# A fused encoder layer on one core: the S5 tap products issued strip by strip, or round the four column strips

## The chip, the cores and the metric

The kernel runs on one core of a Trainium2 chip (trn2). A core has five engines that run side by side, each in the order of its own instruction stream: TensorE (PE in the profile, with PEld for its weight loads), VectorE (DVE), ScalarE (ACT), GpSimd (POOL) and SyncE (SP), which only issues DMAs here. They wait for each other through semaphores. The metric is the time of one execution on the device in microseconds (us).

## The reference, cut to what matters

The layer has a parallel mixer (an S5 state-space branch and a gated MLP branch, merged by gates), cross-attention to 256 memory tokens, and a SwiGLU feed-forward part, for 512 tokens of width 1024. The change is in the S5 branch:

```
def s5_scan(u, lam_re, lam_im, log_step, b_re, b_im, c_re, c_im, reverse):
    lam = lax.complex(lam_re, lam_im)
    step = jnp.exp(log_step)[:, None]
    lam_bar = jnp.exp(lam * step)
    b_bar = ((lam_bar - 1.0) / lam)[..., None] * b
    bu = jnp.einsum('gpc,lbgc->lbgp', b_bar, u)
    _, states = lax.associative_scan(_linear_recurrence, (a, bu), axis=0, reverse=reverse)
    return jnp.einsum('gcp,lbgp->lbgc', c, states).real

y = d * u
for direction, reverse in ((0, False), (1, True)):
    y = y + s5_scan(u, ..., reverse)
y = gelu(y); y = y * sigmoid(y @ w_glu)
```

There are 32 groups of 16 channels, each with 64 complex states and two directions.

## The kernel before, in words

**Stages.** The dense products of the layer are cut into blocks of weights of 512 KB. Each block is loaded into `wraw` (SP), split into two parts `whi` and `wlo` by ScalarE and VectorE (`split`, L83 to L89), and multiplied on TensorE in three products per pair (`mm3`, L355; `product`, L1101). A plan (`next_w`, L330) loads blocks a few steps ahead. In order: the projections of the input (tiles `pt` and `pf`), the merge products (`bx`, `bq`, `qv`), GLU, output projection, attention, feed-forward.

**The S5 branch beside it.** It is a generator (`s5_program`, L937) that is advanced by `tick` (L453) after each block of dense products, so that its small work on VectorE, ScalarE and GpSimd is traced between the dense blocks. Work that is to come a little later is put off with `later(n, fn)` (L443), n counted in steps of 5.2 us. The sequence is split into 64 chunks of 8 steps. Within a chunk, the branch is a convolution with 15 taps of 16 x 16 per group; across chunks, a scan (`s5_scan`, L893) carries the states.

**The taps.** The 32 groups are taken in four octets of 8 groups. For an octet, `s5_kernels(o)` (L781) lets VectorE form two tiles `e`, the real part (i = 0) and the imaginary part (i = 1), each 128 partitions (64 states x 2 directions) by 8 groups by 8 steps by 16 channels (L790 to L797). Then `products()` (L800) runs:

- GpSimd clears two tiles `bd` (L804), ScalarE copies the input matrices in (L807).
- TensorE forms the taps in a PSUM tile `pk` of 128 x 2 x 128 (L809 to L819). The octet has two quads (q) of four groups (j). Group j of a quad writes only the 32 PSUM partitions from 32j on, with weights of 32 columns, that is one of four column strips of the array (`tile_position=(0, 32 * j)`). Per group there are four products in plain fp32: a wide one (128 columns of `e`, L814) for i = 0 and i = 1, and a narrow one (16 columns, L817) for i = 0 and i = 1, which adds one tap of the other direction on top. All four add into the same strip, the first with `start`, the last with `stop`.
- `store` (L822) copies the taps to `ks` on ScalarE (L827), adds the skip term on VectorE (L828). `spill` (L831) writes them to DRAM as `kd` by DMAs of SP and GpSimd (L835, L836), and `load` (L839) reads them back as `tt` in another arrangement by eight DMAs (L843; on GpSimd's queue for octets 0 and 1, on SP's for 2 and 3).

`s5_outputs(o)` (L904) needs `tt` and the scanned states: ScalarE copies the states to `ss` (L916, L917), TensorE forms `py` (L922 to L924), ScalarE applies the GELU to `y` (L929), and eight DMAs store `yd` (L932). The tiles `tt`, and `y` with `ks`, have one buffer each; `e`, `bd` and `ss` have two. `s5_inputs` (L851) uses transposes (`pw`, L864) and products (`pz`, L871) on the way to the scan. In the program's order the octets 0 and 1 have their taps before the scan; octet 2's are formed after the outputs of octet 0, octet 3's after those of octet 1.

**Who sets the order.** A scheduler orders each engine's instructions when the kernel is built, by its own timing model: an instruction whose operands it takes to be ready may go ahead of others that were traced earlier, or fall behind them. `in_order` (L93, `keep_in_program_order`) ties an instruction behind the instruction of its engine that was traced just before it. It fixes the order of issue and waits for nothing. On the chip every engine then keeps the order that was built. Before the change the tap products have no such tie. In the traced order an octet's first tap product stands directly behind the last dense product of the step before.

Of the kernel before, what the change touches and what calls it, by code (L numbers as in the profile page):

```python
# [27 lines left out]
C = 16  # L28
# [11 lines left out]
Q = 8  # L40
# [12 lines left out]
def hybrid_layer_kernel(  # L53
# [8 lines left out]
    nc = tc.nc  # L62
# [14 lines left out]
    def bank(name):  # L77
        return pm.tile([P, 512], F32, tag="mm", name=name)

    def aux(name, shape=(P, 512)):  # L80
        return pa.tile(list(shape), F32, tag="aux", name=name)
# [11 lines left out]
    in_order = tc.keep_in_program_order  # L93
# [349 lines left out]
    def later(n, fn):  # L443

        side["later"].append((side["now"] + n, fn))
# [321 lines left out]
    def inner(t, gs, n):  # L767

        return t[:, gs, :].unsqueeze(3).to_broadcast([P, GO, t.shape[2], n])

    def outer(t, gs, n):

        return t[:, gs, :].unsqueeze(2).to_broadcast([P, GO, n, t.shape[2]])

    def lc(t, g):
        return t[:, g].rearrange("p a b -> p (a b)")

    def glc(t):
        return t.rearrange("p g a b -> p (g a b)")

    def s5_kernels(o):  # L781

        gs = slice(o * GO, (o + 1) * GO)
        cr, ci = st["c"]
        pr, pi = st["pe"]
        es = []
        for i in range(2):
            e = s5p.tile([P, GO, Q, C], F32, tag="e%d" % i, name="e%d" % i, bufs=2)
            w = s5p.tile([P, GO, Q, C], F32, tag="etmp", name="etmp")
            V.tensor_tensor(e, outer(cr, gs, Q), inner((pr, pi)[i], gs, C), ALU.mult)  # L790
            yield 1.1
            V.tensor_tensor(w, outer(ci, gs, Q), inner((pi, pr)[i], gs, C), ALU.mult)
            yield 1.1
            if i == 0:
                V.tensor_tensor(e, e, w, ALU.subtract)
            else:
                V.scalar_tensor_tensor(glc(e), glc(e), -1.0, glc(w), ALU.mult, ALU.subtract)  # L797
            es.append(e)
            yield 1.1
        def products():  # L800
            bd = []
            for i in range(2):
                t = s5p.tile([P, GO, 2, C], F32, tag="bd", name="bd", bufs=2)
                nc.gpsimd.memset(t, 0.0)  # L804
                for d in range(2):
                    hf = slice(64 * d, 64 * d + 64)
                    nc.scalar.copy(t[hf, :, d, :], st["b"][i][hf, gs, :])  # L807
                bd.append(t)
            ps = aux("pk", (P, 2, P))  # L809
            for q in range(2):  # L810
                for j in range(4):
                    g = 4 * q + j
                    for i in range(2):
                        nc.tensor.matmul(ps[32 * j:32 * j + 32, q, :], bd[i][:, g].rearrange("p d c -> p (d c)"),  # L814
                                         lc(es[i], g), start=(i == 0), stop=False, tile_position=(0, 32 * j))
                    for i in range(2):
                        nc.tensor.matmul(ps[32 * j:32 * j + C, q, 0:C], bd[i][:, g, 1, :],  # L817
                                         es[i][:, g, Q - 1, :], start=False, stop=(i == 1),
                                         tile_position=(0, 32 * j))  # L819
            later(0.5, lambda: store(ps))  # L820

        def store(ps):  # L822
            ks = s5p.tile([P, 2, P], F32, tag="y", name="ks")
            dd = s5p.tile([P, 2, C], F32, tag="dd", name="dd", bufs=2)
            in_order(V.tensor_tensor(dd, st["dmask"].unsqueeze(1).to_broadcast([P, 2, C]),
                                     st["dcol"][:, 2 * o:2 * o + 2].unsqueeze(2).to_broadcast([P, 2, C]), ALU.mult))
            nc.scalar.copy(ks, ps)  # L827
            V.tensor_tensor(ks[:, :, 0:C], ks[:, :, 0:C], dd, ALU.add)  # L828
            later(0.5, lambda: spill(ks))

        def spill(ks):  # L831
            kd = dp.tile([GO, C, 15, C], F32, name=f"kd{o}")
            for j in range(4):
                kdj = kd.rearrange("(q j) c l e -> j c q (l e)", j=4)[j]
                (nc.gpsimd, nc.sync)[o > 1].dma_start(kdj[:, :, 7 * C:15 * C], ks[32 * j:32 * j + C])  # L835
                nc.gpsimd.dma_start(kdj[:, :, 0:7 * C], ks[32 * j + C:32 * j + 2 * C, :, 0:7 * C])  # L836
            later(1.2, lambda: load(kd))

        def load(kd):  # L839
            tt = s5p.tile([P, GO, P], F32, tag="tt", name="tt")  # L840
            kf = kd.rearrange("g c l e -> c g (l e)")
            for l in range(Q):
                (nc.gpsimd, nc.sync)[o > 1].dma_start(tt[l::Q], kf[:, :, (7 - l) * C:(15 - l) * C])  # L843
            st["oct", o] = (es[0], es[1], tt)

        later(1, products)
        yield 0.1

# [211 lines left out]
    for h in range(H):  # L1060
        ps = bank("psv")
# [56 lines left out]
    def unit_bank(name):  # L1118
        return bank(name).rearrange("p (j t) -> p j t", j=2)
# [367 lines left out]
    for t0 in (0, 2):  # L1487
        ps = {t: bank(f"pt{t - t0}") for t in (t0, t0 + 1)}
# [77 lines left out]
    ps = [bank("pf0"), bank("pf1")]  # L1566
# [67 lines left out]
    for i, u in enumerate(UNITS):  # L1634
        final = i == len(UNITS) - 1
        x, v = begun
        q = unit_bank("pq")
# [132 lines left out]
    for i in range(2):  # L1770
        p = aux("pcut", (P, 256))
# [37 lines left out]
```

## Time and profile before

| | us |
|---|---|
| time, median of 3 runs | 893.77 (893.14 to 894.84) |
| span of the profiled execution, first to last instruction | 891.3 |
| TensorE busy in it | 881.1 (99%) |
| VectorE busy | 642.5 (72%) |
| ScalarE busy | 487.4 (55%) |
| wide tap products (L814), 128 on the chip, first and last start | 65.1 to 290.8 |
| narrow tap products (L817), 128 on the chip, first and last start | 69.1 to 291.0 |

The profile has no separate time for the profiled execution beside its span; the median of the runs lies 2.4 us above the span. A line of the timeline gives the start and the length in us, the engine, the line of the kernel, the operation, what it writes and reads, the shape, and a count where equal neighbours are merged; brackets hold the idle time of the engine just before it and what ended it. The lengths of matrix products are modelled and overlap, so starts are what to compare.

### The profile page before, as it was taken

The numbers are of one execution on the slowest core, as the hardware profiler recorded it, in microseconds if no ns is written. First come the engines' busy times: TensorE is split into PE (matmuls) and PEld (weight loads), VectorE is DVE, ScalarE is ACT, GpSimd is POOL, SyncE is SP. The second block draws the span as 40 slices with busy tenths as digits, with TensorE's granted clock in tenths as the row PEclk, the third lists the DMA queues.
The fourth block names the chain that finished last, engine by engine and source line by source line (L and its number), as shares of the span: only waits on it lengthen the run. The fifth ranks groups of instructions, "written<-read, shape, count | busy, mean of one in ns | idle before, by whom it ended". The sixth has DMA issues, their size and how long they took to land.

```text
span 891.3 us, 14796 instructions
## 1 busy us (share of the span) xinstructions
PE 881.1 (99%) x5744; PEld 788.0 (88%) x5744; DVE 642.5 (72%) x1048; ACT 487.4 (55%) x714; POOL 106.9 (12%) x165
## 2 busy tenths in 40 slices
PE   9999999999999999999999999999999999999996
PEld 6788888888889998889899978999999999988875
DVE  5697653889847368658856836676878777899875
ACT  5743994244396254347656534645555455655664
POOL 1005301111032111001001001101121111000010
PEclk9999999999999999999999999999999999999998
DMA  8667456978533789834579747627899999356672
GB/s 255 196 189 182 114 155 177 189 191 190 159 87 84 212 285 268 288 117 140 168 221 256 194 103 197 166 81 181 213 237 233 216 225 249 95 167 207 204 230 102
DMA packets 118408, 165.36 MB, mean 186 GB/s; under 512 B 11825, under 2 KB 84161, under 8 KB 118210
## 3 DMA queue, kind: packets, MB, share of 16 engines
q1 hardware_dynamic: 97474, 135.74, 47.9%
q0 software_dynamic: 20576, 28.15, 19.9%
q8 instruction: 45, 0.74, 0.3%
q10 hardware_dynamic: 288, 0.52, 0.2%
q14 instruction: 25, 0.20, 0.1%
HBM read 157.61 MB, written 46.63 MB: 229 GB/s over the span
## 4 chain that ended last, share of the span: by engine, by line
PE 97%; DMA 1%; SPq 1%; ACT 0%; DVE 0%; issue 0%; POOLq 0%; ACTq 0%
PE pf L358 26%; PE pt L358 17%; PE px L1110 12%; PE dx L358 6%; PE pq L1110 6%; PE dq L358 3%; PE pv L1110 3%; PE bx L1110 3%; PE qx L1110 2%; PE dv L358 2%; PE pz L871 2%; PE pk L814 2%; PE bq L1110 1%; PE qv L1110 1%; PE psc L358 1%; PE qq L1110 1%
## 5 line engine op out<-in xcount | busy, mean ns | idle before, releaser
L86 DVE TENSOR_TENSOR wlo<-wraw,whi 128x1024 fp32r<-128x1024 f32 (+1 forms) x145 | 172.2, 1189 | 101.2 <-ACT whi L85 101.0
L85 ACT CAST whi<-wraw 128x1024 fp32r<-128x1024 f32 (+1 forms) x145 | 148.6, 1026 | 152.2 <-PE pf L358 44.0
L358 PE MATMUL pf<-xn,whi 128*128 128x512 f32 x448 | 139.6, 391 | 0.0
L358 PEld LDWEIGHTS pf<-xn,whi 128*128 128x128 f32 x448 | 83.7, 188 | 17.0
L358 PE MATMUL pf<-xn,wlo 128*128 128x512 f32 x224 | 87.3, 390 | 0.0
L1110 PE MATMUL px<-fn,whi 128*128 128x256 f32 x480 | 83.4, 277 | 0.0
L1110 PEld LDWEIGHTS px<-fn,whi 128*128 128x128 f32 x480 | 72.7, 188 | 0.2
L85 ACT CAST whi<-b 128x1024 fp32r<-128x1024 f32 x40 | 42.2, 1055 | 50.4 <-PE px L1110 27.4
L86 DVE TENSOR_TENSOR wlo<-b,whi 128x1024 fp32r<-128x1024 f32 x40 | 48.9, 1223 | 27.0 <-ACT whi L85 27.0
L1110 PE MATMUL px<-fn,wlo 128*128 128x256 f32 x240 | 66.4, 277 | 0.0
L1110 PE MATMUL pq<-s,whi 128*128 128x256 f32 x320 | 55.0, 276 | 0.0
L358 PE MATMUL dx<-whi,s 128*128 128x512 f32 x170 | 53.4, 390 | 0.4 <-DVE h L1734 0.4
L85 ACT CAST whi<-t 128x1024 fp32r<-128x1024 f32 x30 | 31.6, 1054 | 35.6 <-PE pv L1110 12.4
L86 DVE TENSOR_TENSOR wlo<-t,whi 128x1024 fp32r<-128x1024 f32 x30 | 36.7, 1225 | 19.7 <-ACT whi L85 19.7
L358 PEld LDWEIGHTS pf<-xn,wlo 128*128 128x128 f32 x224 | 42.1, 188 | 8.7
L1110 PEld LDWEIGHTS pq<-s,whi 128*128 128x128 f32 x320 | 48.3, 188 | 0.0
L1110 PEld LDWEIGHTS px<-fn,wlo 128*128 128x128 f32 x240 | 45.1, 188 | 0.0
L358 PE MATMUL pt<-whi,xn 128*128 128x512 f32 x128 | 43.7, 412 | 0.7 <-ACT xn L85 0.7
L1110 PE MATMUL pq<-s,wlo 128*128 128x256 f32 x160 | 44.2, 276 | 0.0
L358 PEld LDWEIGHTS dx<-whi,s 128*128 128x128 f32 x170 | 31.8, 188 | 7.5 <-issue 0.8
L358 PE MATMUL dx<-wlo,s 128*128 128x512 f32 x85 | 33.0, 390 | 0.0
L275 POOL DMA_DIRECT2D dsum<-in_w_down_dram x12 | 13.3, 1105 | 162.4 <-DMA dsum<-in_w_down_dram 162.4
(453 smaller groups left out, 2296.8 us busy)
## 6 DMA issues: line engine op xcount, KB each, us to landing
wraw<-in_w_in_dram SPq DMA_DIRECT2D x36, 512.0 KB, 4.7
dsum<-in_w_down_dram SPq DMA_DIRECT2D x20, 512.0 KB, 5.4
wraw<-dsum SPq DMA_DIRECT2D x20, 512.0 KB, 4.1
b<-in_w_gate_dram SPq DMA_DIRECT2D x15, 512.0 KB, 5.4
b<-in_w_up_dram SPq DMA_DIRECT2D x15, 512.0 KB, 5.3
wraw<-in_w_down_dram SPq DMA_DIRECT2D x15, 512.0 KB, 4.4
dsum<-in_w_down_dram POOLq DMA_DIRECT2D x10, 512.0 KB, 8.1
dsum<-dsum POOLq DMA_DIRECT2D x10, 512.0 KB, 8.5
```

The source lines that it names most:

```text
L85: hi = nc.scalar.copy(dst_hi, src)
L86: lo = nc.vector.tensor_tensor(dst_lo, src, dst_hi.bitcast(F32), ALU.subtract)
L275: plan[j + step][1].append((0, lambda d=dst, x=more: nc.gpsimd.dma_start(d, x, accum_op=ALU.add)))
L358: m = nc.tensor.matmul(ps, a[x], b[y], start=start and i == 0, stop=stop and i == 2, skip_group_check=free)
L814: nc.tensor.matmul(ps[32 * j:32 * j + 32, q, :], bd[i][:, g].rearrange("p d c -> p (d c)"), lc(es[i], g), start=(i == 0), stop=False, tile ...
L871: nc.tensor.matmul(ps[:, g, :], wt[:, g, :], u[:, o * GO + g, :], start=True, stop=True)
L1110: nc.tensor.matmul(ps[:, j, :], a[x], b[y], start=start and j == k == i == 0, stop=k == 3 and i == 2, skip_group_check=True)
```

## The change

The loops over the groups j and over the two parts i change places, for the wide and for the narrow products separately, and every product is tied to the program's order. Before, the four products of one strip follow each other and then the next strip comes. After, the wide products of i = 0 go round the four strips, then those of i = 1, then the narrow ones of i = 0, then those of i = 1; then the second quad does the same. Number, shapes, operands and the sums in each strip stay.

```
             ps = aux("pk", (P, 2, P))
             for q in range(2):
-                for j in range(4):
-                    g = 4 * q + j
-                    for i in range(2):
-                        nc.tensor.matmul(ps[32 * j:32 * j + 32, q, :], bd[i][:, g].rearrange("p d c -> p (d c)"),
-                                         lc(es[i], g), start=(i == 0), stop=False, tile_position=(0, 32 * j))
-                    for i in range(2):
-                        nc.tensor.matmul(ps[32 * j:32 * j + C, q, 0:C], bd[i][:, g, 1, :],
-                                         es[i][:, g, Q - 1, :], start=False, stop=(i == 1),
-                                         tile_position=(0, 32 * j))
+                for i in range(2):
+                    for j in range(4):
+                        g = 4 * q + j
+                        in_order(nc.tensor.matmul(ps[32 * j:32 * j + 32, q, :], bd[i][:, g].rearrange("p d c -> p (d c)"),
+                                                  lc(es[i], g), start=(i == 0), stop=False, tile_position=(0, 32 * j)))
+                for i in range(2):
+                    for j in range(4):
+                        g = 4 * q + j
+                        in_order(nc.tensor.matmul(ps[32 * j:32 * j + C, q, 0:C], bd[i][:, g, 1, :],
+                                                  es[i][:, g, Q - 1, :], start=False, stop=(i == 1),
+                                                  tile_position=(0, 32 * j)))
             later(0.5, lambda: store(ps))
```

## The prediction

> **What bounds the kernel now.** I began with the page: span, busy time, clock and the chain that ended last.
>
> ```profile
> span 891.3 us, 14796 instructions
> PE 881.1 (99%) x5744; PEld 788.0 (88%) x5744; DVE 642.5 (72%) x1048; ACT 487.4 (55%) x714; POOL 106.9 (12%) x165
> ...
> PEclk9999999999999999999999999999999999999998
> ...
> PE 97%; DMA 1%; SPq 1%; ACT 0%; DVE 0%; issue 0%; POOLq 0%; ACTq 0%
> ```
>
> TensorE is busy for 881 of 891 us at a full clock, and 97% of the chain is its own work. A microsecond taken from its stream shortens the kernel until some later product has to wait for an operand that did not get faster. So two things are to be found: what the changed products cost on TensorE, and where the next wait comes. The first answer starts from the view of the tile pk, which holds the tap products.
>
> ```profile
> L814 PE MATMUL pk<-e,bd x128: 272/273/297, 65.1 to 290.8; 128*32 128x128 f32 x128
> ...
> L817 PE MATMUL pk<-e,bd x128: 176/176/179, 69.1 to 291.0; 128*16 128x16 f32 x128
> ...
> who waited for it (us, times):
>   POOL bd L804: 13.2, 3
>   ACT ks L827: 7.5, 1
> ```
>
> The code has 64 wide products (L814) and 64 narrow ones (L817), 16 of each in an octet; the trace has 128 of each, so the chip runs every fp32 product as two. The 273 ns are no cost, because products overlap; the cost is read from starts, in the timeline of TensorE in the first octet.
>
> ```profile
> 68.53 0.39 PE L358 MATMUL pt<-wlo,xn 128*128 128x512 f32 x1
> 68.85 0.41 PE L814 MATMUL pk<-e,bd 128*32 128x128 f32 x2
> 69.09 0.18 PE L817 MATMUL pk<-e,bd 128*16 128x16 f32 x1
> ...
> 69.56 0.18 PE L817 MATMUL pk<-e,bd 128*16 128x16 f32 x1
> 69.56 0.30 PE L814 MATMUL pk<-e,bd 128*32 128x128 f32 x1
> 69.59 0.23 PE L817 MATMUL pk<-e,bd 128*16 128x16 f32 x3
> 69.70 0.49 PE L814 MATMUL pk<-e,bd 128*32 128x128 f32 x3
> 70.03 0.18 PE L817 MATMUL pk<-e,bd 128*16 128x16 f32 x1
> ...
> 72.36 0.26 PE L817 MATMUL pk<-e,bd 128*16 128x16 f32 x4
> 72.54 0.50 PE L358 MATMUL pt<-whi,xn 128*128 128x512 f32 x1
> ```
>
> One strip's turn is four wide and four narrow halves. The first narrow half of a turn starts at 69.09, 69.56, ... 72.36, eight times at (72.36 - 69.09) / 7 = 0.467 us, so an octet's eight turns take 3.73 us. Inside a turn three wide halves spread over 0.49 - 0.273 = 0.217 us: 0.108 from start to start. Three narrow ones spread over 0.23 - 0.176: about 0.026 each.
>
> The row that decides is the wide half at 69.56. In the code it is the first of the next strip and stands behind all four narrow halves of the strip before; yet it starts with the first of these, and the other three start at 69.59, inside it. So two strips do run at once. And it slows nobody: its second half starts 0.134 later, 0.108 of streaming and 0.026 that I take for its own uncovered weights. It does not start earlier still, while the older strip's wide halves stream. TensorE thus looks only a few instructions ahead, and a turn of sixteen (eight loads, eight products) in one strip fills its view.
>
> **The change, part by part.** It removes and adds no instruction; the 32 products of an octet stay, and each strip still gets its own in the same order. What moves is the order between strips: now the strip changes after every fp32 product, that is after two loads and two halves, and only four instructions stand between a strip and the next.
>
> *Cost of an octet.* If the four strips run side by side, each has eight wide halves of 0.108 and eight narrow ones of 0.026: 0.86 + 0.21 = 1.07 us, the low end. If no two starts anywhere may be closer than the narrow ones' 0.026, the 64 wide and narrow halves take 64 x 0.026 = 1.66 us, the high end for strips that overlap. I take 1.3: the pair at 69.56 stands nearer to the low end, but the short view will now and then leave a strip without its next weights. Saved per octet: 3.73 - 1.3 = 2.43 us (2.07 to 2.66). No trace of before shows wide halves of two strips side by side; the end without it is the first rival.
>
> A rule of the Trainium skill speaks against this. "TensorE: Matmul & The Clock Gate", section "Part 3: Packing small matmuls", says that matmuls start and end strictly in order, and that weight loads pass running matmuls only in another row group; all products here use all rows, so by it the loads would not overlap and the saving would be nothing or less. The rows at 69.56 and 69.59 contradict it on starts. The same section gives 2.38 times for three column strips, by which the sum would be an estimate of 3.73 / 2.38 = 1.6 us.
>
> *The pin.* Each product is tied behind the TensorE instruction that was issued just before it in the program. It is an order of issue, no wait on a semaphore, so nothing new is queued behind it. Today the first product of three octets goes alone ahead of the rest, because it needs only the real half of the operands:
>
> ```profile
> 263.18 0.41 PE L814 MATMUL pk<-e,bd 128*32 128x128 f32 x2
> 263.52 0.39 PE L1110 MATMUL bx<-yb_hi,whi 128*128 128x256 f32 x1
> ```
>
> Now the four real products of the first quad can go there, in four strips, for about the same 0.34 us, and the rest shrinks by as much. I cost the pin at nothing.
>
> *Who profits at once.* In octets 0 and 1 (65 to 82 us) the other engines stand and wait for these products:
>
> ```profile
> 72.65 0.37 ACT L827 COPY ks<-pk 128x256 f32<-128x256 f32 x1 [7.48 <-PE pk L817]
> 72.69 0.56 POOL L804 MEMSET bd<- 128x256 f32 x2 [4.11 <-PE pk L817]
> ...
> 73.06 0.20 DVE L828 TENSOR_TENSOR ks<-ks,dd 128x32 f32<-128x32 f32 x1 [1.76 <-ACT ks L827]
> ```
> ```profile
> 82.11 0.56 POOL L804 MEMSET bd<- 128x256 f32 x2 [4.50 <-PE pk L817]
> ...
> 84.28 1.23 DVE L885 TENSOR_TENSOR wsx<-bbr,pw 128x1024 f32<-128x1024 f32 x1 [3.74 <-PE pw L864]
> ```
>
> VectorE's idle time here, 1.76 + 3.74 = 5.50 us, covers what two octets save, 4.86, so the conversions and the S5 chain move with TensorE. The scan that follows starts from TensorE's results; it moves as a whole. Octets 0 and 1 give 2 x 2.43 = 4.86 us to the end.
>
> *What is late next.* Octets 2 and 3 lie behind the scan. There the outputs of octet 2 (tile py, L922) need the taps tt, which have gone through DRAM:
>
> ```profile
> 273.30 0.62 ACT L85 CAST s<-zf 128x512 fp32r<-128x512 f32 x1
> 275.25 1.13 ACT L916 COPY ss<-zh 64x504 f32<-64x504 f32 x1 [1.33 <-PE py L924]
> ...
> 279.84 2.00 ACT L85 CAST whi<-wraw 128x1024 fp32r<-128x1024 f32 x2
> 281.86 1.28 ACT L929 ACT_TABLE_LOAD   x1
> 283.15 0.60 ACT L929 ACTIVATE y<-py 128x512 f32<-128x512 f32 x1
> ```
> ```profile
> 283.78 2.62 SPq L932 DMA_DIRECT2D yd<-y  x4
> 286.44 3.12 SPq L843 DMA_DIRECT2D tt<-kd  x5
> ```
> ```profile
> DMA to landing us min/median/max: 2.1/2.6/6.0
> ```
> ```profile
> 291.49 0.41 PE L922 MATMUL py<-u,tt 128*128 128x64 f32 x2
> ```
>
> The five last tt loads stand on SP's queue behind the stores of y, which wait for ScalarE's y at 283.15. The last is issued at about 289.0 and with 2.6 us lands near 291.5, just when py starts: no slack. ScalarE has no gap from 275.25 to y, and before 275.25 only 1.33 us of idle, which wait for the py products of octet 1 on TensorE. So y, the loads and this py come earlier by the 4.86 of octets 0 and 1 plus 1.33 of what octet 2 saves, and no more; octet 3 gives nothing, its products stand ahead of this py. TensorE will arrive some 9.7 us early and wait about 3 us there.
>
> Behind this py nothing new is late: the next step of the branch waits for TensorE again.
>
> ```profile
> 311.57 0.60 ACT L929 ACTIVATE y<-py 128x512 f32<-128x512 f32 x1 [6.34 <-PE py L924]
> ```
>
> **Sum.** 2 x 2.43 + 1.33, and 0.06 for the slack: 6.25 us off the span of 891.3, which makes 885.1. The median of the runs shown, 893.77, lies 2.4 above the span; that stays, and the forecast is 893.8 - 6.25 = 887.5 us. With the ends of the octet's cost: 2 x 2.07 + 1.4 = 5.5 (888.2) and 2 x 2.66 + 1.4 = 6.7 (887.1).
>
> **The rivals.**
>
> *Wide halves of two strips do not overlap (slower).* The place is the octet itself. What the trace shows beside a wide half is only three narrow ones of 16 columns; four full streams may ask for more than the operand reads give. Then an octet takes 32 x 0.108 + 32 x 0.026 = 4.29 us, 0.56 more than now, since today's order hides three narrow halves of each turn; with 0.026 of uncovered weights at each of 16 changes of strip it is 4.7. Times four: 2.2 to 3.9 us more, 896.0 to 897.7. It decides from the point where an octet exceeds 3.73, that is where wide halves come further apart than (3.73 - 0.83) / 32 = 0.091 on the mean. Against it: the unslowed wide half at 69.56. 0.13. The rule of the Trainium skill quoted above ("TensorE: Matmul & The Clock Gate", "Part 3: Packing small matmuls") would end here.
>
> *Overlap of two only.* If TensorE sees just the next strip's first half while a second half waits, a product costs about 0.108 and the sixteen wide ones 1.8 us, with the narrow ones 2.2 to 2.6. Saved per octet 1.1 to 1.5, about 1.3; the sum 2 x 1.3 + 1.4 = 4.0, so 889.8. For it: the view is short. Against it: four instructions per strip leave room for more than one strip. 0.16.
>
> *The new wait costs clock.* Where TensorE comes out of idleness, at the start, the trace shows half speed:
>
> ```profile
> 10.66 1.05 PE L358 MATMUL pt<-whi,xn 128*128 128x512 f32 x2
> ...
> 13.19 0.62 PE L358 MATMUL pt<-whi,xn 128*128 128x512 f32 x2
> ```
>
> Two products stand 1.05 - 0.63 = 0.42 apart there and 0.23 from 13.19 on. If 3 us of idleness before py bring that back for as long as from 9.6 to 13.2, some 1.7 us are lost: 889.2. Against it: the wait below left no mark on the clock row, but it is shorter. 0.06. The Trainium skill ("TensorE: Matmul & The Clock Gate", "Part 1: The HAM clock gate") puts the limit at an idle window of about 3.4 us, close to this wait.
>
> ```profile
> PE pt L358 <- ACT ot_hi L85: 0.9, 2, 0.7
> ```
>
> *It does not do what it says.* The scheduler could place the pinned products singly between others. Each change between full products and strips costs: 0.34 us for the two halves at 263.18 against 0.22 inside a turn. A handful of such stints, or another order in the crowded stretch from 262 to 292, would eat the gain: about 893.8. 0.07.
>
> **How the numbers follow.** Forecast 0.58, the others as given. A measurement of this kernel can tell about 0.2% (1.8 us) from no change. Faster by more: 0.58 + 0.16 + 0.06 = 0.80; within: 0.07; slower: 0.13. The range reaches below the low end, 887.1, by 0.6, for ScalarE's chain may give a little more than 1.33, and up beyond 889.8 to the weak end of an overlap by two (saved 1.1 at each of three places and a bit: 890.4), with 0.8 for the weights: 886.5 to 891.2 holds 0.80.
>
> **What would show it.** Right: wide halves of different strips start within 0.01 to 0.03 us of each other; an octet's products take 1.1 to 1.7 us from first to last; the waits of ACT ks and POOL bd shrink; a new wait of TensorE on the DMA of tt ahead of L922, 2 to 4 us, behind octet 3; then an even lead of some 6 us to the end. Wrong: wide halves still 0.108 apart across strips; pk in more than two stretches per octet; a granted clock below 1 after that wait; or no such wait and a lead near 10 us, then the S5 chain had slack that I did not see.

## The result and the profile after

| | before | after |
|---|---|---|
| time, median of 4 runs each, us | 894.14 (893.14 to 894.84) | 889.2 (888.54 to 889.93) |
| ratio of after to before | | 0.995, 95% interval 0.9938 to 0.9961 |
| span of the profiled execution, us | 891.3 | 888.2 (its time: 889.93, the longest of the four) |

The change makes the kernel 4.9 us faster; 6.25 had been forecast. In the profile after, lines behind the loop are two higher: L817 is now L819, L827 is L829, L922 is L924, L929 is L931, L1110 is L1112.

First the page of after.

```profile
span 888.2 us, 14796 instructions
...
PE 870.7 (98%) x5744; PEld 776.9 (87%) x5744; DVE 643.3 (72%) x1048; ACT 486.2 (55%) x714; POOL 106.8 (12%) x165
...
PEclk9999999999999999999999999999999999999999
...
PE 89%; DMA 3%; DVE 2%; ACT 2%; SPq 2%; issue 1%; POOL 0%; POOLq 0%; DVEq 0%; ACTq 0%
```

TensorE is busy 881.1 - 870.7 = 10.4 us less, 2.6 per octet, but the span is shorter by only 3.1 (by 4.6 for the shortest of the four, 886.7). So the products got cheaper as wanted, and more than half of that is lost. That the chain fell from 97% to 89% of TensorE says the same: there are now places where the end hangs on a DMA, ScalarE or VectorE.

The saving itself stands in the timeline of TensorE, in octet 1, whose products run in one stretch.

```profile
74.65 0.65 PE L814 MATMUL pk<-e,bd 128*32 128x128 f32 x16
75.11 0.28 PE L819 MATMUL pk<-e,bd 128*16 128x16 f32 x16
...
75.66 0.28 PE L819 MATMUL pk<-e,bd 128*16 128x16 f32 x16
75.86 0.50 PE L358 MATMUL pt<-wlo,xn 128*128 128x512 f32 x1
```

Sixteen wide halves start within 0.65 - 0.27 = 0.38 us; the four that one strip has among them alone took 0.108 each before. An octet takes 75.86 - 74.65 = 1.21 us, where it took 3.73. The view of the tile pk shows the two old waits for these products shrunk (13.2 and 7.5 us before):

```profile
  POOL bd L804: 7.4, 2
  ACT ks L829: 4.7, 2
```

Where does the gain go? The table by stages, with the stretch from the scan's end to the output projection: before, then after. The second number behind the stretch is TensorE's busy time, the third from the end the granted clock (1.00 is full speed).

```profile
245.00:310.00 65.00, 65.00 (x570) 61.62 (x568) 35.29 (x40) 42.37 (x52) 15.98 (x38) 1.00 0.46 123
310.00:345.00 35.00, 35.00 (x223) 31.72 (x223) 23.01 (x27) 17.60 (x24) 4.60 (x7) 1.00 0.94 299
```
```profile
245.00:310.00 65.00, 61.32 (x598) 58.27 (x597) 36.60 (x42) 41.27 (x51) 17.97 (x42) 1.00 0.49 135
310.00:345.00 35.00, 33.78 (x187) 28.63 (x186) 22.55 (x28) 15.52 (x21) 2.51 (x4) 1.00 0.93 288
```

Before, TensorE had not one idle moment there; now it stands 3.68 + 1.22 = 4.9 us. The waits of TensorE from 245 to 340 us name the places (total, times, longest); before had none in this stretch.

```profile
PE py L924 <- DMA tt<-kd: 1.6, 2, 1.2
PE pf L358 <- ACT ya_hi L85: 1.1, 1, 1.1
PE bx L1112 <- ACT u L1130: 1.0, 1, 1.0
PE bq L1112 <- ACT s L85: 0.8, 1, 0.8
PE bq L1112 <- DVE s L86: 0.3, 1, 0.3
```

Only the first of these five was foreseen. Read from starts (how much later than at their usual distance the next products start, which also counts slow starts just behind a wait), they cost 6.4 us: py 0.53 + 1.37, ya 1.25 + 0.57, u 1.15, s 0.95 + 0.61.

The wait for ya is the output projection's, behind GLU. ScalarE's rows there, before and then after:

```profile
329.04 1.28 ACT L1229 ACT_TABLE_LOAD   x1
332.92 0.58 ACT L1229 ACTIVATE pf<-pf 128x512 f32<-128x512 f32 x1 [2.60 <-PE pf L358]
```
```profile
322.16 1.28 ACT L1231 ACT_TABLE_LOAD   x1
328.97 0.58 ACT L1231 ACTIVATE pf<-pf 128x512 f32<-128x512 f32 x1 [5.53 <-PE pf L358]
```

ScalarE is ready 6.9 us earlier, but its first sigmoid comes only 3.95 us earlier: it waits for TensorE, 5.53 us in place of 2.60. GLU has 48 products in four PSUM banks, and a sigmoid needs one bank complete. In the built order of before the first bank is complete after 29 of the 48 products; in that of after the scheduler deals the products out in turn over all four banks, and the first is complete after 39. All four sigmoids then crowd at the end and the projection waits for them. Nobody wrote this order; it is the scheduler's. That its timing model counts the new taps as quicker is an inference from the order that it built.

### The profile page after: what moved, and what is told of

It reads as the page before. It is cut to its first block, busy times and chain, and to the rows that moved or that the text cites. A ratio compares the mean times of both kernels' runs of the same rounds, so it can differ in the third digit from the quotient of the medians.

```text
span 888.2 us, 14796 instructions
## 1 busy us (share of the span) xinstructions
PE 870.7 (98%) x5744; PEld 776.9 (87%) x5744; DVE 643.3 (72%) x1048; ACT 486.2 (55%) x714; POOL 106.8 (12%) x165
## 4 chain that ended last, share of the span: by engine, by line
PE 89%; DMA 3%; DVE 2%; ACT 2%; SPq 2%; issue 1%; POOL 0%; POOLq 0%; DVEq 0%; ACTq 0%
PE pf L358 25%; PE pt L358 17%; PE px L1112 12%; PE pq L1112 6%; PE dx L358 5%; PE dq L358 3%; PE pv L1112 3%; PE qx L1112 2%; PE dv L358 2%; PE pz L873 2%; PE psc L358 1%; PE qq L1112 1%; PE ptr L520 1%; PE po L358 1%; PE bq L1112 1%; DMA slab<-in_s_log_step_dram 1%
## 5 line engine op out<-in xcount | busy, mean ns | idle before, releaser
L1112 PE MATMUL px<-fn,whi 128*128 128x256 f32 x480 | 83.3, 276 | 0.0
L1112 PEld LDWEIGHTS px<-fn,whi 128*128 128x128 f32 x480 | 72.6, 188 | 0.2
L1112 PE MATMUL px<-fn,wlo 128*128 128x256 f32 x240 | 66.4, 277 | 0.0
L1112 PE MATMUL pq<-s,whi 128*128 128x256 f32 x320 | 55.0, 276 | 0.0
L1112 PEld LDWEIGHTS pq<-s,whi 128*128 128x128 f32 x320 | 48.2, 188 | 0.0
L1112 PEld LDWEIGHTS px<-fn,wlo 128*128 128x128 f32 x240 | 45.1, 188 | 0.0
L1112 PE MATMUL pq<-s,wlo 128*128 128x256 f32 x160 | 44.2, 276 | 0.0
```

Of the source, the lines that this page charges most:

```text
L1112: nc.tensor.matmul(ps[:, j, :], a[x], b[y], start=start and j == k == i == 0, stop=k == 3 and i == 2, skip_group_check=True)
```

## The experiments

The theories come in the order in which they were held. **Theory A** (the prediction's): behind the scan, ScalarE's chain and the DMA queue of the branch cap the end, so octets 2 and 3 give almost nothing. Its rival **B**: each octet gives its own share.

**New order in octets 0 and 1 only, and in 2 and 3 only.**

```
+                if o < 2:        # the other kernel: o >= 2
+                    ... wide, then narrow: for i: for j: (tied)
+                else:
+                    ... for j: wide i=0,1, narrow i=0,1 (as before)
```

> New order of the tap products in octets 0 and 1 only; octets 2 and 3 strip by strip as before. Theory A (behind the scan the S5 branch on ScalarE and the DMAs sets the end; what octets 2 and 3 save is waited away): about as fast as the whole change, 4.5 to 5.5 us under before. Theory B (each octet gives its own share, the whole change loses elsewhere): only about half of the whole change's gain, 2 to 3 us under before.

> New order in octets 2 and 3 only. Theory A: no more than 1.4 us under before, and down to nothing, though TensorE's own work shrinks by 5.3 us. Theory B: 2 to 3 us under before or more.

Measured: octets 0 and 1 alone 893.12 us, ratio 1.0003 (0.9988 to 1.0018), nothing; octets 2 and 3 alone 899.23 us, ratio 1.0078 (1.0056 to 1.0099), six us slower. Both theories missed both kernels, A the first by more and B the second. The halves as built do not add up to the whole, so no share can be read off as it stands. TensorE's longest waits from 245 to 350 us for octets 0 and 1 alone (lines behind the taps are 16 higher than before):

```profile
PE pf L358 <- ACT ya_hi L85: 1.1, 1, 1.1
PE bq L1126 <- ACT s L85: 0.8, 1, 0.8
PE bq L1126 <- DVE s L86: 0.3, 1, 0.3
```

and for octets 2 and 3 alone TensorE's timeline at the py of octet 3, its stretch behind that wait, and its timeline at the joint between GLU and projection:

```profile
292.64 0.41 PE L938 MATMUL py<-u,tt 128*128 128x64 f32 x2 [1.13 <-DMA tt<-kd]
```
```profile
294.23:304.47 10.24, 10.24 (x50) 10.24 (x50) 1.23 (x1) 1.64 (x2) 1.87 (x4) 0.50 0.54 170
```
```profile
337.71 0.39 PE L358 MATMUL pf<-yg_hi,wlo 128*128 128x512 f32 x1
341.31 1.07 PE L358 MATMUL pf<-ya_hi,whi 128*128 128x512 f32 x3 [3.21 <-ACT ya_hi L85]
...
343.29 0.63 PE L358 MATMUL pf<-ya_hi,whi 128*128 128x512 f32 x1
343.71 0.63 PE L358 MATMUL pf<-ya_lo,whi 128*128 128x512 f32 x1
...
345.67 0.39 PE L358 MATMUL pf<-ya_hi,whi 128*128 128x512 f32 x1
```

Octets 2 and 3 alone lose at two places. The py of octet 3 waits for tt, 1.3 us by starts, and behind it the granted clock is a half for 10.24 us, in which 5.1 us of work are lost. At the GLU joint the projection stands 3.2 us (3.4 by starts), and then products come 0.43 apart, as at the kernel's start, until 345.4, which loses 1.7. That is 11.5 us lost; the two octets save about half of 10.4, so 6.3 remain, where 6.0 were measured.

In this kernel's build the first GLU bank is complete only after 42 of 48 products; with octets 0 and 1 alone after 39, as in after. Both wait at the GLU joint, the longer the later that bank is complete, and this joint has no wait for the S5 branch in it: ya is made from GLU's own products. For octets 0 and 1 alone the losses in the trace are, by starts, 2.0 us of waits for s and u, 1.8 for ya, and 1.6 of half clock behind that (rows in the last section): 5.4, which is what the two octets had saved. This trace is of the longest of the twelve executions (897.5 us). It reached the first tap product, ahead of every changed one, 3.0 us later than the trace of before did, so its 4.4 us over before are mostly not the change's. The seven executions at a granted clock of 0.997 or more have a median of 892.4, 0.8 under before, where the waits alone would leave 1.6; the rest is open.

**Half of the copies of the scanned states on VectorE**, with the change and without, to shorten ScalarE's chain:

```
-            nc.scalar.copy(s[hi_, :, 0:NCH - 1], zv[hi_, :, 0:NCH - 1][:, :, ::-1])
+            V.tensor_copy(s[hi_, :, 0:NCH - 1], zv[hi_, :, 0:NCH - 1][:, :, ::-1])
```

> The changed kernel, with half of the state copies ss (the upper 64 partitions, line 919 of the changed kernel) on VectorE, which idles at 242 to 251 us, in place of ScalarE. Theory A: ScalarE's chain behind the scan gets up to 4.4 us shorter ahead of the octets 2 and 3, so a part of their 5.3 us comes through: 2 to 4 us under the whole change. If the DMAs of kd and tt alone set the end: within 0.5 us of the whole change. Theory B: within 0.5 us of it as well.

> The same move of copies to VectorE in the kernel before. Both theories: within 0.7 us of before, since TensorE waits for nothing in that stretch there. A gain as large as in the changed kernel would say that the copies matter by themselves, and not as the cap on the octets.

With the change 889.1 us, ratio 0.9952 (0.9934 to 0.9969): in the median as without the copies moved. Before with the copies moved: 893.58, ratio 1.0001 (0.9989 to 1.0013). The median with the change hides two groups: five executions at a granted clock of 0.997 or more took 885.8 to 889.2 us (median 886.0, which is 3.2 under the changed kernel, whose four executions lay at 0.996 to 0.998), and seven at 0.995 or less took 888.6 to 894.1. The trace is of the shortest, 885.81 us; TensorE's waits in it, from 245 to 345 us:

```profile
PE pf L358 <- ACT ya_hi L85: 1.1, 1, 1.1
PE py L924 <- DMA tt<-kd: 1.0, 1, 1.0
PE pf L358 <- ACT yg_hi L85: 1.0, 1, 1.0
```

The waits for s and u are gone, but one for yg has come, and the one for ya is as it was. So ScalarE's copies are one of the things that cost the gain: where the clock held, moving them gave the 2 to 4 us that theory A had named. They are not the cap that A made of them. By A octets 0 and 1 alone had to keep their gain, and they kept nothing; and the wait for ya stays whoever makes the copies.

**Theory C:** the lead is lost at joints where the build, re-sorting with its new timing, has put products ahead of their operands; the largest single one is the GLU order. Its rival **D:** the S5 branch sets the end whatever the order, and TensorE would only wait elsewhere. The test puts one tie into GLU: the first product of the second column block stays behind the last of the first block. TensorE's order ahead of GLU is unchanged by it. Behind GLU it is not: the build re-sorts products as far as the attention. Nor is it the order of before: with the tie the first bank is complete after 22 products in all four kernels, where before had 29.

```
     def mm3(...):
-            if turn:
+            if turn or (head and i == 0):
                 in_order(m)
...
-                feat_block(ps, ws.pop(), act, nk, kpt, slice(0, n))
+                feat_block(ps, ws.pop(), act, nk, kpt, slice(0, n), head=w is w_glu and c0 > 0)
```

> The changed kernel with one tie more: the first GLU product of the second column block stays behind the last one of the first block (as it is nearly without a tie in the kernel before). Nothing else in TensorE's order moves. Theory C (the rest of the lead is lost because the build deals out the 48 GLU products in turn over all four banks, so that the first sigmoid starts late and the output projection waits 1.25 + 0.28 + 0.29 us for ya): the waits for ya ahead of the projection go, 1.8 us come back, ratio to before near 0.9925 to 0.994 (886 to 888 us), and the lead of about 5 us at 320 us reaches the end. Theory D (the S5 branch's own chain, ending with the loads of y, sets the end whatever the order): TensorE waits as long for yg instead, the time stays that of the change, ratio 0.995.

> New tap order in octets 0 and 1 only, with the same GLU tie. Theory C: its waits for ya (1.25 + 0.29 + 0.29) and the half clock behind them (some 8 products 0.2 us late) go, 3.4 us come back: ratio near 0.9965, about 890 us; what then still lacks of octets 0 and 1's 5.4 us are the waits for s ahead of bq, 1.6 us. Theory D: still no gain, ratio 1.000.

> New tap order in octets 2 and 3 only, with the same GLU tie. Theory C: the 6 us that this kernel lost (3.4 us of wait for ya, 0.5 more in the same stretch, and a clock of 0.93 behind it) come back, and what octets 2 and 3 give (0 to 2 us) shows: ratio 0.998 to 1.000. Theory D: still some 6 us slower, ratio 1.007.

> The kernel before with the GLU tie alone. Theory C: its GLU order was nearly that already and had no wait, so nothing changes: ratio 0.999 to 1.001. Theory D: the same. A gain here of over 1 us would say that the tie brings something of its own, and the gains of the other three would have to be read against it.

| with the GLU tie | us | ratio to before (interval) | without it |
|---|---|---|---|
| the change | 885.74 | 0.992 (0.9899 to 0.9941) | 0.995 |
| octets 0 and 1 | 890.0 | 0.9963 (0.9947 to 0.9979) | 1.0003 |
| octets 2 and 3 | 893.94 | 0.9993 (0.9973 to 1.0013) | 1.0078 |
| before | 892.47 | 0.9981 (0.997 to 0.9992) | 1 |

The first three came as theory C had them (the first a little better), and D's 0.995, 1.000 and 1.007 lie outside their intervals. The last gained 1.2 us where C expected none, so up to that much of the others' gain may be the tie's own. With 0.002 taken off for it, D's ratios become 0.993, 0.998 and 1.005: the first is then inside its interval, the second barely outside, and by the times only octets 2 and 3 decide. The traces decide for all three: by D TensorE would wait as long for yg, and with the tie the wait for ya is gone and none longer than 0.3 us stands in its place. ScalarE's and TensorE's rows of the changed kernel with the tie:

```profile
324.61 0.58 ACT L1231 ACTIVATE pf<-pf 128x512 f32<-128x512 f32 x1 [1.55 <-PE pf L358]
```
```profile
330.08 0.39 PE L358 MATMUL pf<-yg_hi,wlo 128*128 128x512 f32 x1
330.31 0.84 PE L358 MATMUL pf<-ya_hi,whi 128*128 128x512 f32 x3
```

The first sigmoid comes 4.4 us earlier than in after, and the projection follows GLU 0.23 us on, without a wait. So C holds for the GLU order; it does not cover the half clock that octets 2 and 3 alone met ahead of GLU.

**What still lacks, on top of the tie.** TensorE still waits there for s, u and tt, 3.7 us by starts. By theory C these waits are what lacks; its rival E has the loads of y as the next cap, so that shorter waits bring nothing. Three kernels: the copies as above, the tt loads of octets 2 and 3 on two queues, and both.

```
             for l in range(Q):
-                (nc.gpsimd, nc.sync)[o > 1].dma_start(tt[l::Q], ...)
+                (nc.gpsimd, nc.sync)[o > 1 and l % 2].dma_start(tt[l::Q], ...)
```

> The changed kernel with the GLU tie and with half of the copies of the scanned states (ss, two of four per octet) on VectorE in place of ScalarE. Theory C (what still lacks is waited away ahead of bq, bx, py for the branch's operands, 3.7 us in the kernel with the tie alone): ScalarE's chain behind the scan is shorter, the build puts bq behind the taps again, the waits fall to 1 to 2 us, ratio 0.988 to 0.990 (883 to 884.5 us). Theory E (with the tie, the loads of y are the next cap): the lead at 300 us grows, but TensorE waits for yg ahead of GLU and the time stays at that of the tie alone, ratio 0.992.

> The changed kernel with the GLU tie and with the eight tt loads of octets 2 and 3 dealt out to SP and GpSimd, four each, in place of all on SP behind the stores of y. As predicted before the run, the SP queue is what py waits for: then the waits of py for tt (0.61 and 0.54 us with the tie alone) go and the time falls by up to 1.1 us, ratio 0.9908. If what precedes the loads sets their landing (the taps' way through ScalarE, VectorE and DRAM), the waits stay, ratio 0.992; the build also puts py eight products earlier, which costs up to as much again.

> Both edits together. Theory C: the sum, ratio 0.987 to 0.989 (882.5 to 884 us). Theory E: no gain beyond the tie alone, 0.992.

Copies: 885.06 us, ratio 0.9908 (0.9882 to 0.9934); queues: 885.33, 0.9908 (0.9887 to 0.9928); both: 882.62, 0.987 (0.9847 to 0.9892). Neither alone can be told from the tie alone (0.992), so neither decides between C and E; both together lie below it, and E falls. With two queues py follows the taps at once,

```profile
284.33 0.28 PE L819 MATMUL pk<-e,bd 128*16 128x16 f32 x16
284.57 0.41 PE L924 MATMUL py<-u,tt 128*128 128x64 f32 x2
```

but the waits for s and u stay, and a new one for yg comes:

```profile
PE bq L1112 <- ACT s L85: 0.8, 1, 0.8
PE bx L1112 <- ACT u L1130: 0.7, 1, 0.7
PE pf L358 <- ACT yg_hi L85: 0.4, 1, 0.4
```

With the copies alone, the waits for s and u go (the build puts bq behind the taps again), but py waits 1.6 us for tt. With both, one wait is left in the whole stretch, 0.6 us:

```profile
PE py L924 <- DMA tt<-kd: 0.6, 1, 0.6
```

This kernel is 11.2 us faster than before (893.86 in its runs). With up to 1.2 of that the tie's own, about all that the taps save on TensorE, 10.4, arrives. It beats both kernels, the changed one by some 0.8% (0.987 against 0.995, each with its own runs of before).

**Two strips in place of four.**

```
+                for js in ((0, 1), (2, 3)):
+                    for f in (wide, narrow):
+                        for i in range(2):
+                            for j in js:
+                                f(q, j, i, True)
```

> Tap products go round two strips (0 and 1, then 2 and 3 of each quad) in place of four; all tied. If strips run side by side and each needs its own stream time (wide halves 0.109 apart, so 0.55 to 0.6 us for a strip's turn), an octet has four turns of pairs: 1.9 us if the next pair's start hides under the narrow halves, to 2.4. If the change's gain is the fixed order and not the number of strips, an octet takes 1.2 us as with four. One look at the time: 887 to 892 us.

One execution took 891.71 us. Octet 1 on TensorE (wide products are L812 here, narrow ones L819):

```profile
76.54 0.63 PE L812 MATMUL pk<-e,bd 128*32 128x128 f32 x8
77.00 0.19 PE L819 MATMUL pk<-e,bd 128*16 128x16 f32 x2
...
77.48 0.19 PE L819 MATMUL pk<-e,bd 128*16 128x16 f32 x2
...
78.61 0.50 PE L358 MATMUL pt<-whi,xn 128*128 128x512 f32 x1
```

An octet takes 78.61 - 76.54 = 2.07 us, and a pair's turn (77.48 - 77.00) 0.48, where a single strip's took 0.467 before. Two strips cost what one costs. With four, a turn is 75.66 - 75.11 = 0.55. So the gain is the number of strips side by side and not the fixed order.

## Why the prediction was right or wrong

The time came out 1.7 us above the forecast and inside the range. That is partly luck: the octets saved more than forecast, the waits cost more, and the two errors have opposite signs.

*The octet: right.* 1.3 us forecast (1.07 to 1.66), 1.21 measured; saved 2.6 per octet by TensorE's busy time, against 2.43. The first two rivals fall: overlap isn't missing, and overlap of two alone would take 2.07. The reading of one row, a wide half that started inside the older strip's narrow ones, carried it. The rule that was set against it, that loads pass only in another row group (the Trainium skill, "TensorE: Matmul & The Clock Gate", "Part 3: Packing small matmuls"), is not what this trace shows: the strips use the same rows, and 16 wide halves with their own loads start in 0.38 us. Its other half, the strict order of starts, was contradicted by the row at 69.56 already.

*The pin: right.* With the new loops and no tie the build gives the same program, instruction for instruction, so there is no run of it. The four real products of the first quad do go ahead in one stint, eight halves in 65.50 - 65.14 = 0.36 us:

```profile
65.14 0.42 PE L814 MATMUL pk<-e,bd 128*32 128x128 f32 x8
65.50 0.50 PE L358 MATMUL pt<-whi,xn 128*128 128x512 f32 x1
```

*Octets 0 and 1 give 4.86 to the end: wrong as put.* Their gain is real, but "the scan moves as a whole" was short. The scan's first row, before and after:

```profile
154.10 0.22 DVE L898 TENSOR_TENSOR sa<-zh,ca 128x64 f32<-128x64 f32 x1 [2.16 <-ACT zh L877]
```
```profile
150.08 0.23 DVE L900 TENSOR_TENSOR sa<-zh,ca 128x64 f32<-128x64 f32 x1 [2.61 <-ACT zh L879]
```

It starts 4.02 us earlier; in the built order six more dense products, 1.4 us, stand ahead of the branch's own. And alone these octets gave nothing at the end, and 3.6 us with the GLU tie.

*Octets 2 and 3 give 1.39, because py of octet 2 will wait some 3 us: this step failed.* The change and octets 0 and 1 alone, both with the tie, differ by 4.3 us in their medians. The row and its queue were right, the price was not:

```profile
286.32 0.41 PE L924 MATMUL py<-u,tt 128*128 128x64 f32 x2 [0.36 <-DMA tt<-kd]
...
301.40 0.41 PE L924 MATMUL py<-u,tt 128*128 128x64 f32 x2 [1.20 <-DMA tt<-kd]
```
```profile
278.69 0.60 ACT L931 ACTIVATE y<-py 128x512 f32<-128x512 f32 x1
```

At octet 2 the wait is 0.36 us and not 3; the larger one, 1.20, is at octet 3. y came 4.46 earlier (283.15 to 278.69) and this py 5.17 (291.49 to 286.32); the prediction had 4.86 + 1.33 = 6.2 for both. I had set TensorE 9.7 us early there by moving before's order forward; in the order that was built it had already stood 2.7 us for s and u. In before, bq ran behind the taps, whose 3.7 us gave s its time; now 24 bq products stand ahead of 28 of the 32 taps. That cover was not in the working, and with the GLU tie the term of 1.39 is some 3 us too small.

*"Behind this py nothing new is late": wrong.* The GLU joint costs 1.8 us by starts in the changed kernel. I had read the next step of the branch, and not what reads the branch's result.

*Rivals.* "Another order in the crowded stretch would eat the gain" stood under the rival that the change doesn't do what it says, with 0.07. The change does what it says, and yet this clause of it took place: in that stretch bq stands ahead of the taps and waits 1.6 us for s. A price of the same kind came further on, at GLU, outside the stretch that was named. "The new wait costs clock" did not come in after (granted clock 0.996 and above in its four executions), but behind the same wait at octet 3 it cost 5.1 us when octets 2 and 3 were changed alone.

*The sum.* 10.4 us saved, not 9.7; 6.4 waited away by starts, not 3.5, which leaves 4.0 to compare with 3.1 in the profiled execution and 4.9 in the medians. The two traces show where the difference arises: the 2600th of TensorE's 5744 products, at 434 us, starts 3.99 us earlier than in before, the 3500th 3.61, the last 3.19, so the lead was the 4.0, and 0.8 of it goes later on. By the medians, the order at GLU takes 889.2 - 885.74 = 3.5 us (2.3 if the tie's own 1.2 is taken off), and the waits for s, u and tt 885.74 - 882.62 = 3.1.

## What to carry to other kernels

Small fp32 products of these shapes in different column strips cost little more than one strip alone, if the program changes strip with every product: look for one early start in the trace, which told here that the order was the obstacle. Where a scheduler orders the engines by its own timing, a quicker step gives another program, and not the same program moved forward: compare the orders joint by joint, above all at a joint where one engine waits for a complete group, and tie that order before you judge the edit. Test the parts of a change alone with care, since each part is re-sorted too and the parts needn't add up. Set the traced execution's own time and clock beside the median before you explain the median from its trace.

## What the runs showed of the hardware

Column strips ran side by side almost without a price. A turn took 0.467 us with one strip (four wide and four narrow halves), 0.48 with two (eight and eight) and 0.55 with four (sixteen and sixteen).

A short wait can cost clock, and not in every execution. Behind the wait of 1.13 us for tt shown above the clock was halved for 10.24 us, behind the one of 3.2 us for 3.41; in the trace of octets 0 and 1 alone, the same followed a wait of 1.1 us for ya:

```profile
337.67 1.35 PE L358 MATMUL pf<-ya_hi,whi 128*128 128x512 f32 x3 [1.09 <-ACT ya_hi L85]
...
339.60 0.63 PE L358 MATMUL pf<-ya_lo,whi 128*128 128x512 f32 x1
...
341.31 1.87 PE L358 MATMUL pf<-ya_hi,whi 128*128 128x512 f32 x4
343.01 0.40 PE L358 MATMUL pf<-ya_lo,whi 128*128 128x512 f32 x1
```

Eight products from 339.60 to 343.01 take 3.41 us, at 0.227 each they would take 1.82: 1.6 lost. In the trace of after, a wait as long at the same place was followed by full speed. The runs of octets 2 and 3 with the tie fall into two groups by their granted clock: four executions at 0.997 or 0.998 took 888.5 to 890.2 us, eight at 0.988 to 0.993 took 893.4 to 897.6, so their median says little about the order alone. Their trace, of an execution at 0.997, has the same wait for tt (1.09 us) and full clock behind it. The two groups differ by about the 5 us that the half clock cost without the tie; that it is the same loss is likely and not shown.

The Trainium skill ("TensorE: Matmul & The Clock Gate", "Part 1: The HAM clock gate") tells of an activity window of about 3.4 us that runs freely, so that it depends on the phase what falls into it. The traces agree: within each, the recorded changes of clock lie whole multiples of 3.413 us apart (317.44 / 93). With octets 0 and 1 alone three of them are at 22.15, 339.59 and 343.00, which is 93 steps and one; with octets 2 and 3 alone five are at 10.92, 294.23, 304.47, 342.02 and 345.43, which is 83, 3, 11 and 1. With octets 0 and 1 alone TensorE stood 2.05 us, by starts, in the one step that ended at 339.59, and the clock fell there. In after the same waits add up to 2.03, but a step ends at 332.07, between them: 1.25 fall before it and 0.78 behind, and the clock stayed. So 2.05 of 3.41 us were enough here and 1.25 were not; the clock fell without a whole step of idleness. The wait for tt is not settled by this: 1.30 of a step with octets 2 and 3 alone, and the clock fell; 1.26 with the tie, and it stayed.
